# The second feed-forward layer: its first pair of hidden tiles by plain products instead of quarter sums, its second half of tokens as one block, and one PSUM pool

## The chip, the cores and the metric

The kernel runs on one core of one Trainium2 chip. The metric is the time of one execution on the device in microseconds. The time before is the median of three runs, 2837.39 us (2834.97 to 2839.1).

## The reference

Two layers of a diffusion transformer on 1024 tokens of width 1024, with a second small stream of 256 context tokens. Each layer is a mixer with a residual and then a gated feed-forward layer (FFN) with a residual, both on a normed and modulated input. The change touches the end of the second layer: its output projection, the norm behind it, and its FFN. In the reference that is

```
x = x + g_m * y                      # y = concat(fourier_mix, gla_output) @ w_out
h = rmsnorm(x, norm_ffn_w) * (1 + sc_f) + sh_f
x = x + g_f * ((silu(h @ w_gate) * (h @ w_up)) @ w_down)
return rmsnorm(x, final_norm_w)
```

with w_out 1024 x 1024 (half of its products lie earlier in the kernel), w_gate and w_up 1024 x 2816, w_down 2816 x 1024, all in float32.

## The kernel before, in words

**Layout.** x lies transposed in SBUF as eight tiles xT[k] of 128 features x 1024 tokens. Each factor of a product is split into a high and a low part of a shorter float (`split`: ScalarE casts the high part at L56, VectorE subtracts it at L57 for the low part), and one product is three matmuls (`mm3`, L49 to L51). XBLK is the pair of token blocks 0 to 511 and 512 to 1023.

**Seven products for eight.** Gate and up of this FFN are computed for two hidden tiles j and j+1 at a time (11 such pairs, j = 0, 2, ... 20) by a scheme of the Strassen kind: the 1024 x 1024 input is taken as four quarters (features 0 to 511 or 512 to 1023 by tokens 0 to 511 or 512 to 1023), and `quad` does seven products of sums of quarters in the order 1, 2, 5, 6, 7, 3, 4. Operands 1, 2, 4 and 5 are the quarters themselves (tiles called mixc and mixd in the trace), 6, 7 and 3 are sums of quarters, kept by `Sums` as tiles s, e and a. Each product has 12 matmuls of 512 columns into one PSUM bank (tile qp), and VectorE adds it up behind (L666; ScalarE copies the first, L677). The weights' sums are made by GpSimd (L619), split, and handed over by `Feed`, whose calls `take` and `ahead` set where in the program that work stands. Between gate and up of a pair lie the products with w_down of the pair before (`down_sums`, tile dn, residual into xT at L316).

**The stretch that is rewritten.** `out_sums` does the remaining half of the output projection (tile op) in three blocks of tokens, 512, 256 and 256 wide, four steps of two output tiles each. After each step `residual` (L316) adds into xT and `Squares.add` squares and sums (L433, L437). Generators are stepped between the steps: `norm_first` for the first block, `norm_second` for each of the other two. They turn the sums of squares into 1/rms (a matmul ss at L444, a diagonal at L447, a broadcast matmul rbc at L452), write the normed input (L457, L458) with its split, and also the sums of quarters 6, 7 and 3 (L470, L487 to L492). The first pair of hidden tiles needs those sums, so gate and up of j = 0 go by `quad` too, interleaved by hand with the last norm (`next(gate)`, `next(late)`, `next(up)`).

**PSUM.** Two pools follow one another. The first, `ps`, is closed behind the output projection (`pss.close()`), the second, `ps2`, opened for the FFN. In both, tag "s" is two tiles of two banks each, which `psum` hands out in halves, tags t, m and o are single banks. In `ps2` the products of `quad` have a tag of their own, "q", of four single banks, that also serves the final norm (`final`, tile ft).

**What sets the order.** A scheduler places each instruction by the order of the program and by its dependencies; it works by tiles. An engine runs its instructions in that order and stands at one whose semaphores are not there yet.

Of the kernel before, what the change touches and what calls it, by code (L numbers as in the profile page):

```python
# [388 lines left out]
class Sums:  # L389
# [5 lines left out]
    def __init__(self, pool):  # L395
        self.pool = pool
        self.s = {}
        raw = [self.new(f"a{i}", F32) for i in range(4)]
        self.a11 = [raw[k // 2][:, k % 2, :] for k in range(4)]
        self.a1s = [raw[2 + k // 2][:, k % 2, :] for k in range(4)]  # L400

    def new(self, tag, dt=F32R):
        return self.pool.tile([P, 2, 512], dt, name=tag, tag=tag, bufs=1)
# [20 lines left out]
class Squares:


    def __init__(self, s, blk):
        self.s, self.blk, self.acc = s, blk, None

    def add(self, xT, k):  # L430
        s, (o, n) = self.s, self.blk
        sq = scratch(s)[:, :n]
        s.nc.scalar.activation(sq, xT[k][:, o:o + n], AF.Square)  # L433
        if self.acc is None:
            self.acc = sq
        else:
            s.nc.vector.tensor_tensor(self.acc, self.acc, sq, ALU.add)  # L437

    def spread(self):

        s, n = self.s, self.blk[1]
        ss = psum(s, "m", "ss")
        for j in range(n // P):
            s.nc.tensor.matmul(ss[:, j:j + 1], self.acc[:, j * P:(j + 1) * P], s.ones[:, :1], start=True, stop=True)  # L444
        r = rsqrt(s, s.np_, ss[:, :n // P], 1.0 / D)
        dg = scratch(s)[:, :n]
        s.nc.vector.tensor_tensor(dg.rearrange("p (n q) -> p n q", n=n // P),  # L447
                                  s.ident.rearrange("p (o q) -> p o q", o=1).to_broadcast([P, n // P, P]),
                                  r.rearrange("p (n o) -> p n o", o=1).to_broadcast([P, n // P, P]), ALU.mult)
        yield  # L450
        self.bc = psum(s, "o", "rbc")[:, :n]
        s.nc.tensor.matmul(self.bc, s.ones, dg, start=True, stop=True)  # L452

    def normed(self, xT, k, l, dst):

        s, (o, n) = self.s, self.blk
        s.nc.vector.scalar_tensor_tensor(dst, xT[k][:, o:o + n], s.acol[l][1][:, k, 0:1], self.bc, ALU.mult, ALU.mult)  # L457
        s.nc.scalar.activation(dst, dst, AF.Identity, bias=s.mod[l][:, 24 + k, 0:1])  # L458


def norm_first(s, sq, xT, hT, S, l):

    yield from sq.spread()
    yield
    for k in range(KT):
        v = (S.a11 if k < 4 else S.a1s)[k % 4]
        sq.normed(xT, k, l, v)
        split(s, hT[k][0][:, :512], hT[k][1][:, :512], v, "pool" if k % 2 else "dve")
        if k >= 4:
            s.nc.gpsimd.tensor_tensor(v, v, S.a11[k - 4], ALU.add)  # L470
        if k % 2:
            yield


def norm_second(s, sq, xT, hT, S, l):

    nc = s.nc
    o, n = sq.blk
    sl = slice(o - 512, o - 512 + n)
    yield from sq.spread()  # L480
    yield
    for k in range(4):
        a, b = scratch(s), scratch(s)
        a21, a22, s1, s2 = a[:, :n], a[:, n:2 * n], b[:, :n], b[:, n:2 * n]
        sq.normed(xT, k, l, a21)
        sq.normed(xT, k + 4, l, a22)
        nc.vector.tensor_tensor(s1, a21, a22, ALU.add)  # L487
        nc.vector.tensor_tensor(s2, s1, S.a11[k][:, sl], ALU.subtract)
        for i, v, eng in ((5, s1, "dve"), (6, s2, "dve"), (4, a22, "pool")):
            split(s, *[x[:, sl] for x in S.operand(hT, i, k)], v, eng)  # L490
        nc.gpsimd.tensor_tensor(S.a11[k][:, sl], S.a11[k][:, sl], a21, ALU.subtract)
        nc.gpsimd.tensor_tensor(S.a1s[k][:, sl], S.a1s[k][:, sl], s1, ALU.subtract)  # L492
        yield


def norm_last(s, hT, S):

    last = scratch(s)
    for k in range(4):
        split(s, *S.operand(hT, 7, k), S.a11[k])  # L500
        yield
    s.nc.scalar.copy(last, S.a1s[3])
    for k in range(4):
        split(s, *S.operand(hT, 3, k), S.a1s[k] if k < 3 else last)
        yield


def early_weights(s, S, w, at):

    raw = s.wp.tile([P, KT, P], F32, name="wraw", tag="wraw", bufs=s.nraw)  # L510
    s.nc.sync.dma_start(raw, w[:, :P].rearrange("(k p) n -> p k n", p=P))
    units = []
    for x in range(2):
        hi, lo = S.early(at + x)
        split(s, hi, lo, raw[:, 4 * x:4 * x + 4, :].rearrange("p k n -> p (k n)"))
        units.append((hi, lo))
    return units


def out_sums(s, w, mix, xT, hT, S, l, order, early):  # L520


    q0, nq = min(order), len(order)
    weights = lambda k: wslab(s, w[q0 * P:(q0 + nq) * P, k * P:(k + 2) * P], nq, 2 * P)

    todo = [((0, 512), (0, 2, 4, 6)), ((512, 256), (2, 4, 6, 0)), ((768, 256), (0, 6, 4, 2))]
    steps = [(b, k0) for b, ks in todo for k0 in ks]
    load = {0: [0, 2], 1: [4], 2: [6], 4: [0], 8: [2]}
    kept = {}
    late = iter(())  # L530
    sq = None
    for i, (blk, k0) in enumerate(steps):
        o, n = blk
        if sq is None or sq.blk != blk:
            if sq is not None:
                late = norm_first(s, sq, xT, hT, S, l) if o == 512 else norm_second(s, sq, xT, hT, S, l)
            sq = Squares(s, blk)
        if i < 3:
            for c in load.get(i, ()):
                kept[c] = weights(c)  # L540
        if i == 9:
            early()
        wh, wl = kept[k0]
        ps = [psum(s, "s", "op") for _ in range(2)]

        for part in (order[:-1], order[-1:]):
            for x in range(2):
                c = slice(x * P, (x + 1) * P)
                for q in part:
                    mm3(s.nc, ps[x][:, :n], (wh[:, q - q0, c], wl[:, q - q0, c]),  # L550
                        (mix[q][0][:, o:o + n], mix[q][1][:, o:o + n]), q == order[0], q == order[-1])
        for x in range(2):
            residual(s, xT, k0 + x, blk, ps[x][:, :n], l, 2)
            sq.add(xT, k0 + x)
            next(late, None)
        if i >= 3:
            for c in load.get(i, ()):
                kept[c] = weights(c)
    for _ in late:
        pass  # L560
    return norm_second(s, sq, xT, hT, S, l)


# [49 lines left out]
def quarters(w, j, first=True):  # L613
# [4 lines left out]
    def job(feed):  # L618
# [3 lines left out]
        if first:  # L622
            for b in (b11, b21):
                feed.unit(b)
                yield 0
# [35 lines left out]
def quad(s, feed, xs, u, out, done, first=None):  # L661
# [21 lines left out]
    feed and feed.ahead()  # L683
    feed = (yield) or feed
# [19 lines left out]
class Hidden:  # L704


    def __init__(self, s, xs):
        self.s, self.xs = s, xs
        self.g, self.h = {}, {}

    def tile(self, tag, bufs=1, dt=F32):
        return self.s.fp.tile([P, 512], dt, name=tag, tag=tag, bufs=bufs)

    def gate(self, feed, first=None):
# [7 lines left out]
        return quad(self.s, feed, self.xs, self.tile("hu", 2), out, done, first)  # L722

    def up(self, feed, first=None):
# [3 lines left out]
        def done(y, x, c):  # L728
            h = self.g[y, x]
            self.s.nc.vector.tensor_tensor(h, h, c, ALU.mult)  # L730
            if self.s.fh:
                self.keep(y, x)

        return quad(self.s, feed, self.xs, self.tile("hu", 2), out, done, first)
# [28 lines left out]
def out_proj(s, w, mix, xT, l, blocks, order, places, behind):  # L763
# [1272 lines left out]
```

## Time and profile before

| | |
|---|---|
| Median of three runs | 2837.39 us |
| The profiled execution | 2844.29 us, span of the records 2842.5 us |
| TensorE busy | 2715.8 us, 96% of the span |
| VectorE, ScalarE, GpSimd busy | 1759.7, 969.4, 343.1 us |
| Granted TensorE clock, mean | 0.981 |
| From the first 256-wide op matmul (2101.55 us) to the first dn matmul (2222.07 us) | 120.52 us |

Times in the traces are microseconds from the start of the span. In a timeline a row has its start, its duration, engine, line, operation and output <- inputs, and in brackets how long the engine had been idle before it and who released it. A matmul's duration overlaps that of the next, so the distance between two starts is its price. In a table by windows each engine has its busy time with the number of instructions in brackets; PEclk is the share of full clock that TensorE was granted.

### The profile page before, as it was taken

The numbers are of one execution on the slowest core, as the hardware profiler recorded it, in microseconds if no ns is written. First come the engines' busy times: TensorE is split into PE (matmuls) and PEld (weight loads), VectorE is DVE, ScalarE is ACT, GpSimd is POOL, SyncE is SP. The second block draws the span as 40 slices with busy tenths as digits, with TensorE's granted clock in tenths as the row PEclk, the third lists the DMA queues.
The fourth block names the chain that finished last, engine by engine and source line by source line (L and its number), as shares of the span: only waits on it lengthen the run. The fifth ranks groups of instructions, "written<-read, shape, count | busy, mean of one in ns | idle before, by whom it ended". The sixth has DMA issues, their size and how long they took to land.

```text
span 2842.5 us, 39083 instructions
## 1 busy us (share of the span) xinstructions
PE 2715.8 (96%) x14761; PEld 2306.9 (81%) x14761; DVE 1759.7 (62%) x3138; ACT 969.4 (34%) x2102; POOL 343.1 (12%) x346
## 2 busy tenths in 40 slices
PE   8999899889999999999999999999997999999998
PEld 3889788777888888888888878788885888888887
DVE  5655677666664544646433474856677766667666
ACT  3442466554411111111111146465245322223222
POOL 0000122221100000000000020312014211112111
PEclk9999999999999999999999999999998999999999
DMA  8545655765132312213211143542641111121212
GB/s 304 163 129 152 183 163 163 216 197 158 59 119 60 97 55 80 85 50 97 82 38 45 38 142 91 144 146 69 188 137 50 53 59 52 45 60 45 67 52 82
DMA packets 265244, 299.59 MB, mean 105 GB/s; under 512 B 33448, under 2 KB 208225, under 8 KB 265057
## 3 DMA queue, kind: packets, MB, share of 16 engines
q1 hardware_dynamic: 265057, 297.10, 34.8%
q8 instruction: 117, 1.92, 0.3%
q14 instruction: 70, 0.57, 0.1%
HBM read 229.14 MB, written 64.49 MB: 103 GB/s over the span
## 4 chain that ended last, share of the span: by engine, by line
PE 79%; DVE 9%; ACT 4%; DMA 4%; issue 2%; POOL 1%; SPq 0%; DVEq 0%; POOLq 0%; ACTq 0%
PE pg L51 7%; PE pg L50 7%; PE pg L49 7%; PE dn L49 6%; PE dn L51 6%; PE dn L50 6%; PE qp L49 5%; PE qp L50 5%; PE qp L51 5%; PE o L1124 2%; DMA adaw<-in_ada_w_dram 2%; PE pt L1094 1%; DVE adaacc L183 1%; PE qk L49 1%; DVE wlo L57 1%
## 5 line engine op out<-in xcount | busy, mean ns | idle before, releaser
L56 ACT CAST whi<-wraw 128x512 fp32r<-128x512 f32 (+2 forms) x317 | 241.1, 765 | 735.5 <-PE dn L50 414.9
L57 DVE TENSOR_TENSOR wlo<-wraw,whi 128x512 fp32r<-128x512 f32 (+2 forms) x317 | 297.1, 939 | 141.0 <-ACT whi L56 139.5
L316 DVE SCALAR_TENSOR_TENSOR xT<-dn,mod,xT 128x512 f32<-128x512 f32 (+1 forms) x448 | 300.2, 685 | 126.0 <-PE dn L51 125.1
L49 PE MATMUL dn<-hhi,whi 128*128 128x512 f32 (+1 forms) x896 | 328.3, 368 | 6.5 <-DVE xT L316 4.9
L50 PE MATMUL dn<-hlo,whi 128*128 128x512 f32 (+1 forms) x896 | 326.7, 365 | 0.0
L51 PE MATMUL dn<-hhi,wlo 128*128 128x512 f32 (+1 forms) x896 | 326.5, 365 | 0.0
L51 PE MATMUL pg<-hh,wlo 128*128 128x512 f32 x688 | 269.2, 391 | 1.0 <-DVE wlo L57 1.0
L49 PE MATMUL pg<-hh,whi 128*128 128x512 f32 x688 | 269.0, 391 | 0.0
L50 PE MATMUL pg<-hl,whi 128*128 128x512 f32 x688 | 268.3, 390 | 0.0
L183 DVE SCALAR_TENSOR_TENSOR adaacc<-adaw,cs,adaacc 128x1024 f32<-128x1024 f32 x140 | 174.9, 1280 | 117.5 <-DMA adaw<-in_ada_w_dram 114.7
L49 PEld LDWEIGHTS dn<-hhi,whi 128*128 128x128 f32 x896 | 168.9, 189 | 39.3 <-DVE xT L316 10.6
L51 PEld LDWEIGHTS dn<-hhi,wlo 128*128 128x128 f32 x896 | 168.9, 188 | 27.1
L50 PEld LDWEIGHTS dn<-hlo,whi 128*128 128x128 f32 x896 | 169.0, 189 | 26.5
L619 POOL TENSOR_TENSOR wraw<-wraw 128x512 f32<-128x512 f32 x88 | 125.3, 1424 | 496.9 <-DVE wlo L57 309.6
L345 ACT ACTIVATE sg<-pg 128x512 f32<-128x512 f32 (+1 forms) x66 | 34.5, 523 | 360.4 <-PE pg L51 360.3
L346 DVE TENSOR_TENSOR sg<-sg,pg 128x512 f32<-128x512 f32 (+1 forms) x66 | 39.2, 593 | 187.8 <-ACT sg L345 187.8
L51 PEld LDWEIGHTS pg<-hh,wlo 128*128 128x128 f32 x688 | 129.4, 188 | 28.6 <-DVE wlo L57 1.8
L50 PEld LDWEIGHTS pg<-hl,whi 128*128 128x128 f32 x688 | 129.5, 188 | 26.0
L49 PEld LDWEIGHTS pg<-hh,whi 128*128 128x128 f32 x688 | 129.5, 188 | 26.0
L275 POOL TENSOR_TENSOR sqacc<-sqacc,sq 128x512 f32<-128x512 f32 (+1 forms) x14 | 17.0, 1217 | 903.9 <-ACT sq L274 902.8
L1051 POOL TENSOR_SCALAR y<-y,sst 128x768 f32<-128x768 f32 (+2 forms) x80 | 71.7, 897 | 261.2 <-DVE sst L1050 133.7
L50 PE MATMUL pg<-hc,whi 128*128 128x256 f32 x344 | 96.7, 281 | 0.0
(625 smaller groups left out, 6734.2 us busy)
## 6 DMA issues: line engine op xcount, KB each, us to landing
adaw<-in_ada_w_dram SPq DMA_DIRECT2D x96, 512.0 KB, 3.9
wraw<-in_ffn_w_gate_dram SPq DMA_DIRECT2D x45, 512.0 KB, 3.9
wraw<-in_ffn_w_up_dram SPq DMA_DIRECT2D x45, 512.0 KB, 3.8
wraw<-in_ffn_w_down_dram SPq DMA_DIRECT2D x44, 512.0 KB, 3.8
wraw<-in_ab_w_in_dram SPq DMA_DIRECT2D x20, 512.0 KB, 6.0
xd<-xT SPq DMA_DIRECT2D x16, 640.0 KB, 6.6
xs<-xd SPq DMA_DIRECT2D x32, 256.0 KB, 3.4
xd<-xs SPq DMA_DIRECT2D x32, 256.0 KB, 2.9
```

The lines of the kernel that those rows point to most:

```text
L49: nc.tensor.matmul(out, wh, xh, start=start, stop=False)
L50: nc.tensor.matmul(out, wh, xl, start=False, stop=False)
L51: nc.tensor.matmul(out, wl, xh, start=False, stop=stop)
L56: s.nc.scalar.copy(hi, src)
L57: (s.nc.gpsimd if eng == "pool" else s.nc.vector).tensor_tensor(lo, src, f32(hi), ALU.subtract)
L183: nc.vector.scalar_tensor_tensor(acc[:, v], w, c, acc[:, v], ALU.mult, ALU.add)
L316: s.nc.vector.scalar_tensor_tensor(xT[k][:, o:o + n], ps, s.mod[l][:, 8 * vec + k, sel:sel + 1], xT[k][:, o:o + n], ALU.mult, ALU.add)
L345: nc.scalar.activation(sg[:, :n], pg[:, :n], AF.Silu)
L346: nc.vector.tensor_tensor(sg[:, :n], sg[:, :n], pu[:, :n], ALU.mult)
L619: sub = lambda out, x, y: feed.s.nc.gpsimd.tensor_tensor(out, x, y, ALU.subtract)
L1051: nc.gpsimd.tensor_scalar(y[:, :256 + xn], y[:, :256 + xn], st[:, 5:6], 1.0, ALU.mult, ALU.mult)
L1124: nc.tensor.matmul(o_ps[:, ba * P:bz * P], vv[:n, kt, :], at(x, sl)[:n, 0, ba:bz, :].rearrange("p b q -> p (b q)"), start=q == 0 and x == ...
```

## The change

1. `out_sums` goes; the output projection is done by `out_proj`, which the other places of the kernel use already, with two blocks of 512 tokens. `Norm.add` is called behind each residual. The weights of the first two steps are read again for the second block, into places where the quarter sums lie later (`S.places`, tiles s0 to s3).
2. Gate and up of j = 0 are plain products (`H.plain`, tile pg, eight products of 24 matmuls each, 192 in place of 168). For the first half of tokens their weights are split early (`early_weights`, tile e, for gate; `whole` for up). For the second half gate and up are interleaved and take the normed tiles in the order 0, 4, 1, 5, 2, 6, 3, 7. The norm of the second block is one of 512 tokens (L459, L464 to L468), and the quarter sums are made behind it, `sums()` and `rest()` in the program.
3. The operand 3 is made from operand 6: a12 + shift - s2, one VectorE instruction.
4. One PSUM pool is left. The tag "q" is gone: a product of `quad` takes a half of a two-bank tile of tag "s" (of which there are two), and `final` takes such a tile for its two halves.

Line numbers move: the adds of `quad` are at L648 after, the copy at L657, ss at L448, the diagonal at L258, rbc at L261, the norm's product at L459.

```diff
 def psum(s, tag, name=None):
     if tag != "s":
-        return s.ps.tile([P, 512], F32, name=name or tag, tag=tag, bufs={"t": 2, "q": 4}.get(tag, 1))
+        return s.ps.tile([P, 512], F32, name=name or tag, tag=tag, bufs=2 if tag == "t" else 1)
...
+    def tile(self, k, dst, hT, eng="dve"):
+        s, (o, n) = self.s, self.blk
+        s.nc.vector.scalar_tensor_tensor(dst, self.xT[k][:, o:o + n], s.acol[self.l][1][:, k, 0:1], self.bc,
+                                         ALU.mult, ALU.mult)
+        hi, lo = [x[:, o:o + n] for x in hT[k]]
+        if eng == "pool":
+            t = scratch(s)
+            s.nc.scalar.activation(t, dst, AF.Identity, bias=self.shift(k))
+            split(s, hi, lo, t, "pool")
+        else:
+            s.nc.scalar.activation(hi, dst, AF.Identity, bias=self.shift(k))
+            s.nc.vector.scalar_tensor_tensor(lo, dst, self.shift(k), f32(hi), ALU.add, ALU.subtract)
+
+def norm_first(s, N, hT, S):
+    N.spread()
     for k in range(KT):
-        v = (S.a11 if k < 4 else S.a1s)[k % 4]
-        sq.normed(xT, k, l, v)
-        split(s, hT[k][0][:, :512], hT[k][1][:, :512], v, "pool" if k % 2 else "dve")
-        if k >= 4:
-            s.nc.gpsimd.tensor_tensor(v, v, S.a11[k - 4], ALU.add)
-        if k % 2:
-            yield
+        N.tile(k, S.raw[k], hT, "pool" if k % 2 else "dve")
...
+            stt(s2, a22, N.shift(k), a11, ALU.subtract, ALU.subtract)
+            split(s, *S.operand(hT, 6, k), s2)
+            stt(a12, a12, N.shift(k + 4), s2, ALU.add, ALU.subtract)
...
 def quad(s, feed, xs, u, out, done):
     def product(i):
-        ws = first.pop(0) if first else feed.take()
-        ps = psum(s, "q", "qp")
+        hi, lo = feed.take()
+        ps = psum(s, "s", "qp")
...
+    def plain(self, ws, hT, y):
+        nc = self.s.nc
+        o = 512 * y
+        for mats in ((0, 1),) if y else ((0,), (1,)):
+            ps = {m: [psum(self.s, "s", "pg") for _ in range(2)] for m in mats}
+            for k in KORDER if y else range(KT):
+                for m in mats:
+                    for x in range(2):
+                        hi, lo = ws[m][x][k // 4]
+                        c = slice(k % 4 * P, k % 4 * P + P)
+                        mm3(nc, ps[m][x], (hi[:, c], lo[:, c]), [h[:, o:o + 512] for h in hT[k]], k == 0, k == KT - 1)
...
-                pt = [psum(s, "q", "ft") for _ in range(2)]
+                pt = psum2(s, "ft")
...
+    def behind(blk):
+        if blk == XBLK[0]:
+            norm_first(s, norms_[blk], hT, S)
+            ws.append(early_weights(s, S, wg))
+
+    out_proj(s, a["cd_w_out"][0], mix, xT, 1, XBLK, [0, 1, 2, 3], S.places(), behind, lambda blk, k: norms_[blk].add(k))
     wps.close()
-    pss.close()
-    s.ps = pool("ps2", space=PSUM)
...
+    H = Hidden(s)
+    sums, rest = norm_second(s, norms_[XBLK[1]], hT, S)
+    H.plain(ws, hT, 0)
+    H.plain(ws, hT, 1)
     dump("x3", xT, T)
-    for _ in norm_last(s, hT, S):
-        feed.ahead()
+    sums()
+    rest()
```

The order of instructions at two places. First, VectorE's order around the norm of the first block (L457 before and L459 after write the normed tile from xT, acol and rbc; L57 and L468 make the low part; L316 is the residual of the output projection's next block). Before:

```order
L457 SCALAR_TENSOR_TENSOR a_19268<-xT_19241,acol_182,rbc 128x512 [waits DMAHW5_49,PE_49]
L316 SCALAR_TENSOR_TENSOR xT_19245<-op,mod_178,xT_19245 128x256 [waits DMAHW0_49,PE_49]
L457 SCALAR_TENSOR_TENSOR a_19268<-xT_19242,acol_182,rbc 128x512
L437 TENSOR_TENSOR nt<-nt 128x256 [waits Activation_49]
L316 SCALAR_TENSOR_TENSOR xT_19246<-op,mod_178,xT_19246 128x256
L57 TENSOR_TENSOR mixc<-a_19268,mixc 128x512 [waits Activation_49]
```

and after, the rows from the first norm product to the next block's first residuals:

```order
L459 SCALAR_TENSOR_TENSOR a_19269<-xT_19243,acol_182,rbc 128x512
L468 SCALAR_TENSOR_TENSOR mixc<-a_19268,mod_178,mixc 128x512 [waits Activation_49]
L459 SCALAR_TENSOR_TENSOR a_19269<-xT_19244,acol_182,rbc 128x512
L468 SCALAR_TENSOR_TENSOR mixc<-a_19269,mod_178,mixc 128x512 [waits Activation_49]
L459 SCALAR_TENSOR_TENSOR a_19270<-xT_19245,acol_182,rbc 128x512
L459 SCALAR_TENSOR_TENSOR a_19270<-xT_19246,acol_182,rbc 128x512
L459 SCALAR_TENSOR_TENSOR a_19271<-xT_19247,acol_182,rbc 128x512
L468 SCALAR_TENSOR_TENSOR mixd<-a_19270,mod_178,mixd 128x512 [waits Activation_49]
L459 SCALAR_TENSOR_TENSOR a_19271<-xT_19248,acol_182,rbc 128x512
L468 SCALAR_TENSOR_TENSOR mixd<-a_19271,mod_178,mixd 128x512 [waits Activation_49]
L316 SCALAR_TENSOR_TENSOR xT_19245<-op,mod_178,xT_19245 128x512 [waits DMAHW0_49,PE_49]
L316 SCALAR_TENSOR_TENSOR xT_19246<-op,mod_178,xT_19246 128x512
```

The residuals of the second block stood between the norm's instructions before; now they stand behind all twelve of them (two L459 rows stand ahead of this piece).

Second, TensorE's order in an up of the steady part, at the seam from product 6 (operand s) to product 7 (operand e), with the numbers of the tiles. Before:

```order
L49 MATMUL qp_20626<-s3_19806,whi_20556 128x512
L50 MATMUL qp_20626<-s3_19806,whi_20556 128x512
L51 MATMUL qp_20626<-s3_19806,wlo_20557 128x512
L49 MATMUL qp_20647<-e0_20020,whi_20577 128x512 [waits Activation_49]
L50 MATMUL qp_20647<-e0_20020,whi_20577 128x512
L51 MATMUL qp_20647<-e0_20020,wlo_20578 128x512 [waits DVE_49]
```

and after:

```order
L49 MATMUL qp_20817<-s3_19946,whi_20749 128x512
L50 MATMUL qp_20817<-s3_19946,whi_20749 128x512
L51 MATMUL qp_20817<-s3_19946,wlo_20750 128x512
L49 MATMUL qp_20817<-e0_19958,whi_20769 128x512 [waits DVE_49,Activation_49]
L50 MATMUL qp_20817<-e0_19958,whi_20769 128x512
L51 MATMUL qp_20817<-e0_19958,wlo_20770 128x512
```

Products 6 and 7 had tiles of their own and now are the halves of one tile, and the first matmul of product 7 has got a wait for VectorE, whose add (L648) reads the first half of that tile.

More of the change, by code (lines that the diff above doesn't have):

```diff
@@ L397, in __init__, with new, places @@
         self.s = {}
[L398 to L403, printed above, removed]
+        raw = [self.new(f"a{i}", dt=F32) for i in range(4)]
+        self.raw = [raw[k // 2][:, k % 2, :] for k in range(KT)]
+    def new(self, tag, shape=(P, 2, 512), dt=F32R):
+        return self.pool.tile(list(shape), dt, name=tag, tag=tag, bufs=1)
+    def places(self):
+        for i in (0, 2):
+            yield [self.new(f"s{i + x}", (P, 4, 2 * P)) for x in range(2)]
     def early(self, i):
@@ L439, in spread @@
     def spread(self):
-        s, n = self.s, self.blk[1]
-        ss = psum(s, "m", "ss")
-        for j in range(n // P):
+        s = self.s
+        ss = psum(s, s.nbanks[0], "ss")
+        for j in range(4):
             s.nc.tensor.matmul(ss[:, j:j + 1], self.acc[:, j * P:(j + 1) * P], s.ones[:, :1], start=True, stop=True)
[L445 to L449, printed above, removed]
@@ L475, in norm_second @@
-def norm_second(s, sq, xT, hT, S, l):
-    nc = s.nc
[L478 to L493, printed above, removed]
@@ L496, in norm_last @@
[L496 to L517, printed above, removed]
@@ L520, in out_sums @@
[L520 to L551, printed above, removed]
-        for x in range(2):
[L553 to L561, printed above, removed]
@@ new lines, in spread, with shift @@
+        r = rsqrt(s, s.np_, ss[:, :4], 1.0 / D)
+        self.bc = psum(s, s.nbanks[1], "rbc")
+        spread(s, s.np_, r, self.bc, dg=scratch(s))
+    def shift(self, k):
+        return self.s.mod[self.l][:, 24 + k, 0:1]
+    def tile(self, k, dst, hT, eng="dve"):
+        s, (o, n) = self.s, self.blk
+        s.nc.vector.scalar_tensor_tensor(dst, self.xT[k][:, o:o + n], s.acol[self.l][1][:, k, 0:1], self.bc,
[8 more added lines that the diff above has]
+            s.nc.vector.scalar_tensor_tensor(lo, dst, self.shift(k), f32(hi), ALU.add, ALU.subtract)
@@ new lines, in norm_first, with norm_second, sums, last @@
+def norm_first(s, N, hT, S):
+    N.spread()
+    for k in range(KT):
+        N.tile(k, S.raw[k], hT, "pool" if k % 2 else "dve")
+KORDER = (0, 4, 1, 5, 2, 6, 3, 7)
+def norm_second(s, N, hT, S):
+    nc = s.nc
+    N.spread()
+    raw = {}
+    for k in KORDER:
+        raw[k] = scratch(s)
+        N.tile(k, raw[k], hT)
+    def sums():
+        both = s.np_.tile([P, 8], F32, name="both")
+        nc.vector.tensor_tensor(both[:, :4], s.mod[N.l][:, 24:28, 0], s.mod[N.l][:, 28:32, 0], ALU.add)
+        stt = nc.vector.scalar_tensor_tensor
+        for k in range(4):
+            a11, a12, a21, a22 = S.raw[k], S.raw[k + 4], raw[k], raw[k + 4]
+            stt(a22, a21, both[:, k:k + 1], a22, ALU.add, ALU.add)
+            nc.gpsimd.tensor_tensor(a21, a11, a21, ALU.subtract)
+            s2 = scratch(s)
+            stt(s2, a22, N.shift(k), a11, ALU.subtract, ALU.subtract)
+            split(s, *S.operand(hT, 6, k), s2)
+            stt(a12, a12, N.shift(k + 4), s2, ALU.add, ALU.subtract)
+    def last():
+        for i in (5, 7):
+            for k in range(4):
+                split(s, *S.operand(hT, i, k), raw[k + 4 if i == 5 else k])
+        keep = scratch(s)
+        nc.scalar.copy(keep, S.raw[7])
+        for k in range(4):
+            split(s, *S.operand(hT, 3, k), S.raw[k + 4] if k < 3 else keep)
+    return sums, last
@@ new lines, in early_weights @@
+def early_weights(s, S, w):
+    ws = [[], []]
+    for half in range(2):
+        raw = s.wp.tile([P, 4, 2 * P], F32, name="wraw", tag="wraw", bufs=s.nraw)
+        s.nc.sync.dma_start(raw, w[512 * half:512 * (half + 1), :2 * P].rearrange("(k p) n -> p k n", p=P))
+        for x in range(2):
+            hi, lo = S.early(2 * half + x)
+            split(s, hi.rearrange("p (k n) -> p k n", k=4), lo.rearrange("p (k n) -> p k n", k=4),
+                  raw[:, :, P * x:P * (x + 1)])
+            ws[x].append((hi, lo))
+    return ws
@@ L621, in job @@
         sub(t, t, b11)
[L622 to L625, printed above, removed]
+        for b in (b11, b21):
+            feed.unit(b)
+            yield 0
         feed.unit(t)
@@ L642, in quarters, with whole, job @@
     return job, loads
+def whole(w, j):
+    loads = [w[512 * x:512 * (x + 1), j * P:(j + 2) * P].rearrange("(k p) n -> p k n", p=P) for x in range(2)]
+    def job(feed):
+        for _ in range(2):
+            raw = feed.raw()
+            for x in range(2):
+                feed.unit(raw[:, :, P * x:P * (x + 1)])
+                if x:
+                    feed.load()
+                yield 0
+    return job, loads
 def rows(w, j):
@@ L658, in rows, with quad @@
     return job, loads
-def quad(s, feed, xs, u, out, done, first=None):
+def quad(s, feed, xs, u, out, done):
     nc = s.nc
@@ L682, in quad @@
     done(0, 0, c)
-    feed and feed.ahead()
-    feed = (yield) or feed
+    feed.ahead()
     p5 = product(5)
@@ L704, with __init__, gate @@
 class Hidden:
-    def __init__(self, s, xs):
-        self.s, self.xs = s, xs
+    def __init__(self, s):
+        self.s = s
         self.g, self.h = {}, {}
     def tile(self, tag, bufs=1, dt=F32):
-        return self.s.fp.tile([P, 512], dt, name=tag, tag=tag, bufs=bufs)
-    def gate(self, feed, first=None):
+        pool = self.s.fh if tag == "hu" else self.s.fp
+        return pool.tile([P, 512], dt, name=tag, tag=tag, bufs=bufs)
+    def gate(self, feed, xs):
         def out(y, x):
@@ L720, in done, with up @@
             self.s.nc.scalar.activation(c, c, AF.Silu)
-        return quad(self.s, feed, self.xs, self.tile("hu", 2), out, done, first)
-    def up(self, feed, first=None):
+        quad(self.s, feed, xs, self.tile("hu", 2), out, done)
+    def up(self, feed, xs):
         def out(y, x):
@@ L728, in done, with times @@
         def done(y, x, c):
[L729 to L734, printed above, removed]
+            self.times(y, x, c)
+            self.keep(y, x)
+        quad(self.s, feed, xs, self.tile("hu", 2), out, done)
+    def plain(self, ws, hT, y):
[5 more added lines that the diff above has]
+                for m in mats:
+                    for x in range(2):
+                        hi, lo = ws[m][x][k // 4]
+                        c = slice(k % 4 * P, k % 4 * P + P)
+                        mm3(nc, ps[m][x], (hi[:, c], lo[:, c]), [h[:, o:o + 512] for h in hT[k]], k == 0, k == KT - 1)
+            for x in range(2):
+                if 0 in mats:
+                    self.g[y, x] = self.tile("ua" if (y, x) == (1, 0) else f"g{y}{x}")
+                    nc.scalar.activation(self.g[y, x], ps[0][x], AF.Silu)
+                if 1 in mats:
+                    self.times(y, x, ps[1][x])
+    def times(self, y, x, c):
+        h = self.g[y, x]
+        self.s.nc.vector.tensor_tensor(h, h, c, ALU.mult)
     def keep(self, y, x):
@@ L760, in down_sums, with out_proj @@
             behind([(o, n)])
-def out_proj(s, w, mix, xT, l, blocks, order, places, behind):
+def out_proj(s, w, mix, xT, l, blocks, order, places, behind, each=None):
     q0, nq = min(order), len(order)
@@ L1765, in dump @@
                 nc.sync.dma_start(dbg[name][k * P:(k + 1) * P, :n], t[:, :n])
-    pss = ctx.enter_context(ExitStack())
-    s.ps = pss.enter_context(P_("ps", space=PSUM))
+    s.ps = pool("ps", space=PSUM)
     s.half = s.bg = None
@@ L1940, in body @@
     feed = Feed(s, jobs + [rows(wd, HT - 2)])
-    next(late)
-    feed.ahead(1)
-    next(up)
-    for _ in late:
-        feed.ahead(1)
+    units = [feed.take() for _ in range(4)]
+    ws.append([[[u.rearrange("p k n -> p (k n)") for u in units[2 * half + x]] for half in range(2)] for x in range(2)])
+    H = Hidden(s)
+    sums, rest = norm_second(s, norms_[XBLK[1]], hT, S)
+    H.plain(ws, hT, 0)
+    H.plain(ws, hT, 1)
     dump("x3", xT, T)
-    for _ in norm_last(s, hT, S):
-        feed.ahead()
+    sums()
+    rest()
     nps.close()
     s.fh = pool("fp3", side="right")
-    H.keep(0, 0)
-    def rest(steps):
-        try:
-            steps.send(feed)
-        except StopIteration:
-            pass
-    rest(gate)
-    rest(up)
+    for y in range(2):
+        for x in range(2):
+            H.keep(y, x)
+    xs = lambda i, k: S.operand(hT, i, k)
     for j in range(2, HT, 2):
-        last, H = H, Hidden(s, xs)
-        for _ in H.gate(feed):
-            pass
+        last, H = H, Hidden(s)
+        H.gate(feed, xs)
         down_sums(s, feed, xT, last.h, 1)
-        for _ in H.up(feed):
-            pass
+        H.up(feed, xs)
     sps.close()
```

57 lines of the change are left out of this document (19 added, 38 removed).

## The prediction

> **What bounds the kernel now.** I read the page first, then stretches of the span, then the timeline at TensorE's gaps, since the page leaves little but TensorE:
>
> ```profile
> span 2842.5 us, 39083 instructions
> PE 2715.8 (96%) x14761; PEld 2306.9 (81%) x14761; DVE 1759.7 (62%) x3138; ACT 969.4 (34%) x2102; POOL 343.1 (12%) x346
> ```
>
> The stretches (after the span of each: its length, then busy time of PE, PEld, DVE, ACT and POOL, the granted clock, DMA):
>
> ```profile
> 2104.83:2136.62 31.79, 26.68 (x183) 24.95 (x183) 28.40 (x50) 19.08 (x38) 14.83 (x11) 0.89 0.12 35
> 2136.62:2151.30 14.68, 0.00 (x0) 0.03 (x1) 12.57 (x23) 6.63 (x18) 11.42 (x12) 0.59 0.23 71
> 2151.30:2181.55 30.25, 25.52 (x86) 17.60 (x86) 23.71 (x41) 15.61 (x35) 15.76 (x19) 0.86 0.06 18
> 2205.20:2813.00 607.80, 607.80 (x2685) 503.02 (x2684) 418.93 (x575) 168.70 (x283) 112.14 (x79) 1.00 0.18 53
> ```
>
> The last row is the steady part: TensorE has no gap in 607.8 us, 607.80 / 2685 = 0.2264 us for a matmul of 512 columns, at full clock. Whatever the change adds in waits there is paid in full. The three rows above are the rewritten stretch; it holds gaps and half clock. Its ends, its largest gap and the row that ends it:
>
> ```profile
> 2101.55 0.28 PE L49 MATMUL op<-mixc,whi 128*128 128x256 f32 x1
> 2101.67 0.28 PE L50 MATMUL op<-mixc,whi 128*128 128x256 f32 x1
> 2150.73 0.47 DVE L457 SCALAR_TENSOR_TENSOR nt<-xT,acol,rbc 128x256 f32<-128x256 f32 x1
> 2151.30 0.77 PE L49 MATMUL qp<-mixc,e 128*128 128x512 f32 x1 [14.69 <-issue]
> 2222.07 0.39 PE L49 MATMUL dn<-hhi,whi 128*128 128x512 f32 x1
> ```
>
> The stretch takes 2222.07 - 2101.55 = 120.5 us. The first qp starts 0.10 us after the last L457 of the second block has ended (2150.73 + 0.47): that instruction is the last reader of rbc, a tile of the pool that is closed here, so the 14.69 us is the pool's change waiting for the second block's norm. The other waits of TensorE in it, from the view of waits and the timeline:
>
> ```profile
> PE ss L444 <- DVE nt L437: 2.3, 1, 2.3
> PE qp L50 <- DVE mixc L57: 2.9, 3, 1.0
> 2117.42 0.48 DVE L316 SCALAR_TENSOR_TENSOR xT<-op,mod,xT 128x256 f32<-128x256 f32 x1
> 2117.95 0.39 PE L49 MATMUL op<-mixc,whi 128*128 128x256 f32 x1 [1.99 <-DVE xT L316]
> ```
>
> The last two also give the restart: 2117.95 - 2117.90 = 0.05 us from VectorE's end to the next matmul. Work without gaps would be 192 x 0.12 (2101.55 to 2101.67) + 252 x 0.2264 (168 of j = 0, 84 of the gate of j = 2) + about 4 for ss and rbc = 84 us; 36 us are lost.
>
> **The rewritten stretch after.** Matmuls: 96 op, 192 pg and the 84 of the next gate, all of 512 columns: 372 x 0.2264 = 84.2 us. The plain products cost 24 matmuls (5.4 us) more than the sevenfold scheme; the blocks of 512 cost 21.7 in place of 23.0. Prices for the rest:
>
> ```profile
> 2127.17 0.58 PE L444 MATMUL ss<-ones,nt 128*128 128x1 f32 x4 [2.32 <-DVE nt L437]
> 2163.54 0.70 PE L452 MATMUL rbc<-nt,ones 128*128 128x256 f32 x2 [0.89 <-DVE nt L447]
> 2117.81 1.40 DVE L457 SCALAR_TENSOR_TENSOR a<-xT,acol,rbc 128x512 f32<-128x512 f32 x2
> L57 DVE TENSOR_TENSOR wlo<-wraw,whi 128x1024 fp32r<-128x1024 f32 x2 | 2.4, 1214 | 0.0
> ```
>
> - ss and rbc, two norms: 2 x (0.58 + 0.70) and some 0.3 of draining at each of the four: 4 us, an estimate, as before.
> - First ss: two 1024-wide low parts of 1.21 us stand on VectorE ahead of the last residuals and sums of squares; between nothing and 2.4, I take 1.4. The two rbc wait for rsqrt and diagonal, 0.89 in the row; I take 0.7 each.
> - The third op step of the second block takes the two-bank tile whose last reader is the residual of xT5. In VectorE's order that residual, the second of two, stands behind all twelve instructions of the first norm: 14 x 0.70 = 9.8 us after rbc. TensorE has 26 matmuls left by then, 5.9 us. The stall is 3.9 us, and what is queued behind it are all later op and pg matmuls. Bounds: 0, if VectorE keeps ahead (it does not stand elsewhere), and 6, if the low parts on it wait for ScalarE.
> - A gap of that size costs half a clock window (3.43 us at half clock, see below): 1.7, between 0 and 3.4.
> - The pool's change is gone, and pg of the first half needs only the first norm, done by then. The second norm (8 x 0.70, low parts, ss without stall) lies beside 96 pg matmuls, 21.7 us. Its sums, with their low parts some 40 instructions of VectorE of 0.7 us, 28 us, lie beside the second 96 (21.7 us) and the products 1, 2 and 5 of the next gate (36 matmuls, 8.2 us). That cover of 30 us is thin; the next gate's product 6 is what would be late. I put 0.3 there, between 0 and 6.
>
> Sum: 84.2 + 4 + 1.4 + 1.4 + 3.9 + 1.7 + 0.3 = 96.9 us against 120.5: **23.6 us less**, between 16 and 32.
>
> **The steady part after.** Here the change of tags tells. In an up of the present kernel, at the ends of products 6 and 7 (TensorE and VectorE rows of the timeline, then the whole group):
>
> ```profile
> 2314.32 0.39 PE L51 MATMUL qp<-s,wlo 128*128 128x512 f32 x1
> 2314.55 0.39 PE L49 MATMUL qp<-e,whi 128*128 128x512 f32 x1
> 2314.75 0.69 DVE L666 TENSOR_TENSOR hu<-qp,hu 128x512 f32<-128x512 f32 x1 [0.48 <-PE qp L51]
> 2317.04 0.39 PE L51 MATMUL qp<-e,wlo 128*128 128x512 f32 x1
> 2317.27 0.39 PE L49 MATMUL qp<-a,whi 128*128 128x512 f32 x1
> 2317.47 0.69 DVE L666 TENSOR_TENSOR hu<-qp,hu 128x512 f32<-128x512 f32 x1 [0.49 <-PE qp L51]
> L666 DVE TENSOR_TENSOR hu<-qp,hu 128x512 f32<-128x512 f32 x58 | 40.0, 689 | 44.6 <-PE qp L51 44.5
> ```
>
> Product 7 starts 0.23 us after the last matmul of 6, beside the add. If it must wait for the add, it starts at 2314.75 + 0.69 + 0.05 = 2315.49 and not at 2314.55: 0.94 us lost. The same at the next seam: 2317.47 + 0.69 + 0.05 - 2317.27 = 0.94. VectorE stood idle ahead of both adds, so nothing delays them now.
>
> Which seams wait: 14 products of a gate and an up fill seven tiles, and the tiles in an up are (4 of the gate, 1), (2, 5), (6, 7), (3, 4). Product 7 writes the tile that the add of 6 reads; the tile (3, 4) goes where the add of 7 has just freed one. Both have no other matmul between. With ten ups that is 20, less two in the last up, where dn matmuls stand between: 18 x 0.94 = 16.9 us. Of those two, one has two matmuls between (0.94 - 2 x 0.2264 = 0.5). Some 31 further waits (2 to 5, 7 to 3 in the gates, the dn behind) have four matmuls between, 0.91 of 0.94 us: 0.03 each, or 0.2 where VectorE is at another instruction: 3. The start of each gate behind product 4's add, with six between: 0.15 each, 1.5. Sum: **22 us more**. Bounds: 15 (the 18 alone, some of them covered) and 30 (each add 0.4 late behind a low part of the weights).
>
> Its loads are two fewer (before two early and four by `Feed` for j = 0, after two and two; six for the projection in both): hidden, DMA being 0.18 busy in the steady row. GpSimd loses its quarter sums (12% busy in all): nothing waits for it there. The S4 instruction is one VectorE instruction of 0.7 us for a GpSimd add: in the sums above.
>
> **The tail.** `final` takes one tile for two halves, so the transposes of the second half wait for the square of the first:
>
> ```profile
> L1685 ACT ACTIVATE fsq<-ft 128x512 f32<-128x512 f32 x16 | 9.4, 596 | 20.7 <-PE ft L1683 14.6 <-issue 6.1
> ```
>
> Eight tiles at 0.6 us, most with other matmuls between, the last ones not: 1 us, between 0 and 3.
>
> **Sum.** -23.6 + 22 + 1 = -0.6 us. The profiled execution took 2844.29, 6.9 above the median; the sum is a difference, and I set it against the median: 2837.39 - 0.6, 2837 us. For this kernel 0.2% is 5.7 us, about what a measurement can tell from no change.
>
> **A rule that speaks against the change.** The clock as the trace shows it, in three neighbouring windows of 3.43 us:
>
> ```profile
> 2166.66:2170.09 3.43, 2.22 (x9) 1.15 (x7) 3.43 (x7) 1.48 (x4) 2.04 (x3) 1.00 0.00 0
> 2170.09:2173.52 3.43, 2.01 (x7) 0.93 (x6) 3.43 (x7) 2.20 (x5) 2.42 (x3) 1.00 0.00 0
> 2173.52:2176.95 3.43, 3.43 (x9) 2.20 (x8) 3.03 (x6) 2.97 (x7) 1.86 (x4) 0.50 0.00 0
> ```
>
> A window with 2.22 us of PE work left the next at full clock, one with 2.01 us brought half clock. In the steady part after, two seams are 12 matmuls (2.7 us) apart, so no window holds more than one whole gap: 3.43 - 0.8 = 2.6 us of work, above both. I take full clock. The Trainium skill, "TensorE: Matmul & The Clock Gate", section "A second HAM failure mode: psum-queue depth-cycling", says otherwise of a kernel that cycles through PSUM banks: the small idles between groups of matmuls were frequent enough to make the clock swing between half and full. By that rule the time would be that of rival 3.
>
> **The rivals.**
> 1. Faster, the wait is not on the add. The order marks that product 7 waits for VectorE, not for which instruction; were it an older one (a low part of weights), the 18 seams cost nothing. For: the order before shows such marks at product 3, with no gap. Against: 6 and 7 write one tile, and dependencies go by tiles. -23.6 + 5 + 1: 2820 us.
> 2. Faster, the stretch runs without its stalls: no 3.9, no 1.7, no 2.8 at the norms. For: VectorE was 28.4 of 31.8 us busy with the old, longer list. Against: the residual stands where the order shows it. 8.4 less: 2828 us.
> 3. Slower, the clock swings in the steady part: each up loses one half-clock window, 1.7 us, ten times: 2837 + 17 = 2854 us. It decides if a window with 2.6 us of work is counted as idle; the first row above speaks against it.
> 4. Slower, VectorE is the bound at the seams and in the sums: adds start 0.4 late behind low parts of weights (8 us at 20 seams), and the second gate's product 6 waits 3 us for its operands: 2848 us. For: the thin cover of 30 us. Against: the idle 0.48 us ahead of the adds.
> 5. The change does not take the gap away but moves it to the third op step: 3.9 becomes 14 if that step also waits for its reloaded weights, queued behind the early gate weights: 2848 us. Against: these loads are issued in the first block.
>
> **How the numbers follow.** Chances: forecast with its bounds (2828 to 2846) 0.60; rival 1 0.08, rival 2 0.12, rival 3 0.07, rivals 4 and 5 0.13 together. The forecast's own spread puts about 0.43 within 0.2%, 0.08 below and 0.09 above. With the rivals: faster 0.08 + 0.08 + 0.12 = 0.28; slower 0.09 + 0.07 + 0.13 = 0.29; same 0.43. The range of 2825 to 2851 leaves out rivals 1 and 3 and a little at the ends, under 2 in 10.
>
> **What would show it.** In the trace after: no gap of 14 us at the output projection's end; one of about 4 us ahead of an op matmul, released by L316; the first dn some 97 us behind the first op matmul of the second block; in each up two gaps of 0.75 us on TensorE ahead of qp with e and with a, released by L648; the clock at 1.00 in the steady part. I am wrong if those gaps are missing or larger than 1 us, if the clock falls there, or if the gate of j = 2 stands for its operands s, e or a.

## The result and the profile after

The changed kernel takes 2872.32 us, median of four runs (2871.06 to 2875.75), against 2838.18 for the kernel before on the same chip: a ratio of 1.0124, 95% interval 1.0107 to 1.0142. It is 34 us slower; 2837 with a range to 2851 was forecast. Its profiled execution took 2872.18 us, span 2870.2.

The same three stretches by windows (columns as above: length, busy time of PE, PEld, DVE, ACT, POOL, clock, DMA). Before, the rewritten stretch, the steady part and the tail:

```profile
2101.55:2222.07 120.52, 95.71 (x468) 77.89 (x466) 100.02 (x162) 61.14 (x123) 53.06 (x47) 0.89 0.16 48
2222.07:2812.54 590.47, 590.47 (x2606) 488.61 (x2605) 404.30 (x555) 161.30 (x270) 107.36 (x76) 1.00 0.18 52
2812.54:2842.50 29.96, 20.49 (x161) 18.44 (x159) 20.07 (x49) 10.33 (x32) 4.34 (x8) 0.89 0.38 141
```

After, from the first op matmul of the second block to the first dn, on to the first ft, and to the end:

```profile
2091.91:2195.08 103.17, 90.80 (x370) 71.72 (x368) 75.09 (x104) 42.42 (x71) 20.37 (x14) 0.93 0.09 29
2195.08:2840.47 645.39, 608.74 (x2628) 489.30 (x2629) 386.73 (x561) 165.33 (x274) 107.46 (x76) 1.00 0.16 49
2840.47:2870.20 29.73, 20.95 (x161) 18.72 (x159) 20.43 (x49) 10.80 (x32) 4.36 (x8) 0.87 0.38 142
```

After, dn begins ahead of the gate's last two products, so 24 matmuls (5.4 us) have moved from the first row to the second. Like for like the stretch takes 103.2 + 5.4 = 108.6 us, 11.9 less than before; the steady part 645.4 - 5.4 = 640.0, **49.5 more**; the tail 0.2 less. That is +37.4, of which the medians show 34. The stretch begins at 2101.55 in the one execution and at 2091.91 in the other, though TensorE has 11531 instructions ahead of it in both: that part varies by some us from execution to execution (its mean granted clock was 0.98 in the one and 0.99 in the other), which is why stretches and not spans are compared here.

Who kept TensorE waiting in the steady part, in the view of waits after (sum, times, longest):

```profile
PE qp L49 <- DVE hu L648: 15.8, 18, 0.9
PE qp L49 <- ACT hu L657: 10.7, 9, 1.3
PE qp L49 <- DVE ua L648: 9.7, 10, 1.0
```

The first row is what the prediction counted, 18 gaps at the seams 6 to 7 and 7 to 3. One of them in the timeline:

```profile
2299.67 0.39 PE L51 MATMUL qp<-s,wlo 128*128 128x512 f32 x1
...
2300.10 0.69 DVE L648 TENSOR_TENSOR hu<-qp,hu 128x512 f32<-128x512 f32 x1
...
2300.94 0.47 PE L49 MATMUL qp<-e,whi 128*128 128x512 f32 x1 [0.88 <-DVE hu L648]
```

From start to start it is 1.27 us in place of 0.23. The other two rows were not foreseen. The seam from 2 to 5 in an up, GpSimd to TensorE:

```profile
2291.90 1.29 POOL L586 TENSOR_TENSOR wraw<-wraw 128x512 f32<-128x512 f32 x1 [0.69 <-DVE wlo L57]
...
2292.97 0.39 PE L51 MATMUL qp<-mixd,wlo 128*128 128x512 f32 x1
...
2293.22 1.14 ACT L56 CAST whi<-wraw 128x512 fp32r<-128x512 f32 x2 [1.96 <-POOL wraw L586]
...
2293.88 0.69 DVE L57 TENSOR_TENSOR wlo<-wraw,whi 128x512 fp32r<-128x512 f32 x1 [2.12 <-ACT whi L56]
2294.49 0.68 DVE L648 TENSOR_TENSOR ua<-qp,hu 128x512 f32<-128x512 f32 x1
...
2295.23 0.50 PE L49 MATMUL qp<-mixc,whi 128*128 128x512 f32 x1 [0.97 <-DVE ua L648]
```

(The two casts, and likewise other rows marked x2 or more, are merged in this view.) Product 2 was done at 2293.36 (2292.97 + 0.39). Its add stood on VectorE behind a low part of weights, that behind its cast, that behind GpSimd's sum of weights. The add ended at 2295.17, and product 5, the other half of the same tile, started then. Four matmuls in between (0.9 us) did not cover it. The same at the seam from 1 to 2 in a gate, with ScalarE's copy as the reader (ten matmuls of product 5 in between):

```profile
2314.95 0.62 ACT L56 CAST whi<-wraw 128x512 fp32r<-128x512 f32 x1 [2.63 <-POOL wraw L586]
2315.47 0.61 ACT L56 CAST hhi<-hu 128x512 fp32r<-128x512 f32 x1
2315.99 0.57 ACT L657 COPY hu<-qp 128x512 f32<-128x512 f32 x1
2316.62 0.50 PE L49 MATMUL qp<-mixd,whi 128*128 128x512 f32 x1 [1.17 <-ACT hu L657]
```

The adds are not later than they were. In the kernel before, the same add:

```profile
2308.88 0.39 PE L51 MATMUL qp<-mixd,wlo 128*128 128x512 f32 x1
2309.11 0.39 PE L49 MATMUL qp<-mixc,whi 128*128 128x512 f32 x1
...
2309.79 0.69 DVE L57 TENSOR_TENSOR wlo<-wraw,whi 128x512 fp32r<-128x512 f32 x1 [2.12 <-ACT whi L56]
2310.40 0.68 DVE L666 TENSOR_TENSOR ua<-qp,hu 128x512 f32<-128x512 f32 x1
```

It started 1.13 us after its product had ended, as after (2294.49 - 2293.36), behind the same cast; product 5 had a bank of its own and started at 2309.11. Four tiles hid this lateness, and the change uncovered it.

In the stretch, the larger gaps after are 2.0 us ahead of ss, and these two (each with the VectorE instruction that, as read below, ended it):

```profile
2113.35 2.71 DVE L316 SCALAR_TENSOR_TENSOR xT<-op,mod,xT 128x512 f32<-128x512 f32 x4
...
2114.85 0.76 PE L49 MATMUL op<-mixc,s 128*128 128x512 f32 x1 [4.64 <-ACT whi L56]
...
2156.63 1.27 DVE L735 TENSOR_TENSOR g<-g,pg 128x512 f32<-128x512 f32 x2
...
2157.95 0.50 PE L49 MATMUL pg<-mixc,whi 128*128 128x512 f32 x1 [3.68 <-DVE g L735]
```

The op step starts some 0.1 us after the second of the four residuals (2113.35 + 2 x 0.68 = 2114.71). The row names a cast on ScalarE that ended 0.3 us before the step (it started at 2113.94), but that cast is of weights of w_up, which the step does not read; the last experiment comes back to this. The pg of the second half waits for the last reader of a pg tile of the first half, a multiply that stands on VectorE behind the second norm and the first of the quarter sums.

### The profile page after: what moved, and what is told of

It reads as the page before. It is cut to its first block, busy times and chain, and to the rows that moved or that the text cites. A ratio compares the mean times of both kernels' runs of the same rounds, so it can differ in the third digit from the quotient of the medians.

```text
span 2870.2 us, 38742 instructions
## 1 busy us (share of the span) xinstructions
PE 2721.8 (95%) x14687; PEld 2292.9 (80%) x14687; DVE 1722.3 (60%) x3090; ACT 959.6 (33%) x2058; POOL 311.5 (11%) x313
## 5 line engine op out<-in xcount | busy, mean ns | idle before, releaser
L56 ACT CAST whi<-wraw 128x512 fp32r<-128x512 f32 (+2 forms) x309 | 234.8, 767 | 743.7 <-PE dn L50 406.0
L316 DVE SCALAR_TENSOR_TENSOR xT<-dn,mod,xT 128x512 f32<-128x512 f32 (+1 forms) x448 | 299.9, 686 | 122.1 <-PE dn L51 121.2
L57 DVE TENSOR_TENSOR wlo<-wraw,whi 128x512 fp32r<-128x512 f32 (+2 forms) x309 | 280.3, 912 | 149.5 <-ACT whi L56 149.3
L51 PEld LDWEIGHTS dn<-hhi,wlo 128*128 128x128 f32 x896 | 168.9, 188 | 27.5 <-DVE wlo L57 0.4
L586 POOL TENSOR_TENSOR wraw<-wraw 128x512 f32<-128x512 f32 x80 | 113.5, 1418 | 552.5 <-DVE wlo L57 381.9
L51 PE MATMUL pg<-hc,wlo 128*128 128x256 f32 x344 | 96.7, 281 | 0.0
```

Source lines behind the costliest of these rows:

```text
L51: nc.tensor.matmul(out, wl, xh, start=False, stop=stop)
L56: s.nc.scalar.copy(hi, src)
L57: (s.nc.gpsimd if eng == "pool" else s.nc.vector).tensor_tensor(lo, src, f32(hi), ALU.subtract)
L316: s.nc.vector.scalar_tensor_tensor(xT[k][:, o:o + n], ps, s.mod[l][:, 8 * vec + k, sel:sel + 1], xT[k][:, o:o + n], ALU.mult, ALU.add)
L586: sub = lambda out, x, y: feed.s.nc.gpsimd.tensor_tensor(out, x, y, ALU.subtract)
```

## The experiments

Theory A: the loss is qp products sharing two-bank tiles, and the rest of the change is a gain. Theory B: the steady part is slower for another reason. For the seams nobody had foreseen, C1: the reader stands in its queue behind weights that GpSimd has not summed; C2: VectorE and ScalarE have too much to do.

**The change without its PSUM part.**

```diff
-        return s.ps.tile([P, 512], F32, name=name or tag, tag=tag, bufs=2 if tag == "t" else 1)
+        return s.ps.tile([P, 512], F32, name=name or tag, tag=tag, bufs={"t": 2, "q": 4}.get(tag, 1))
-        ps = psum(s, "s", "qp")     # pg and ft likewise
+        ps = psum(s, "q", "qp")
     wps.close()
+    pss.close()
+    s.ps = pool("ps2", space=PSUM)
```

> The changed kernel with the PSUM of before for the FFN: the first pool closed behind the output projection, the second with four single banks "q" for qp, pg and ft. Theory A (all of the loss is qp products sharing two-bank tiles, and the rest of the change gains what the stretch shows, 21.6 us): no gap in the steady part, 2838 - 21.6 and 0 to 5 us for the pool's change, 2816 to 2822 us. Theory B (the steady part is slower for another reason, the phase of the weight feed or the places of tiles in SBUF, and the seams only show it): gaps stay under other names, 2850 us or more.

Measured: 2822.00 us, ratio to before 0.9936 (0.9921 to 0.9951). Stretch and steady part:

```profile
2091.55:2198.00 106.45, 95.68 (x394) 75.72 (x392) 78.82 (x108) 43.11 (x72) 23.44 (x14) 0.94 0.10 30
2198.00:2788.47 590.47, 590.47 (x2606) 488.61 (x2604) 405.15 (x557) 162.43 (x273) 107.50 (x76) 1.00 0.18 53
```

The steady part is to the hundredth that of before, without a gap. Theory A holds, B falls: with the weight feed and the places as changed, banks of their own in a second pool are enough. The stretch is worth 120.5 - 106.5 = 14.1 us. (The 21.6 in the expectation was counted from 2101.55 in both executions and is wrong by the 9.6 us by which the stretch began earlier. With 14.1 in its place the range would have been 2824 to 2829, so that the time lies on the upper end of the one written down, 2822, is luck; the medians put the gain at 16.7.)

**The PSUM part alone, on the kernel before.**

```diff
-        ps = psum(s, "q", "qp")     # ft likewise
+        ps = psum(s, "s", "qp")
-    pss.close()
-    s.ps = pool("ps2", space=PSUM)
```

> The kernel before with one edit: one PSUM pool, qp and ft in halves of two-bank tiles. Theory A: the steady part loses the same 47 us and the tail 2; the 14.7 us gap of the pool's change and its half clock go, but the quads of j = 0 get seam waits of their own: 2838 + 49 - 18 + 0 to 15, 2868 to 2884 us. Theory B: the steady part stays without gaps, 2820 to 2838 us.

Measured: 2901.48 us, ratio 1.0226 (1.0204 to 1.0248).

```profile
2105.74:2233.28 127.54, 98.04 (x444) 76.09 (x442) 97.43 (x157) 59.29 (x119) 53.26 (x47) 0.84 0.14 42
2233.28:2881.59 648.31, 609.14 (x2629) 488.94 (x2628) 389.41 (x560) 165.37 (x274) 107.89 (x76) 1.00 0.16 48
```

The steady part loses 648.3 - 5.4 - 590.5 = 52.4 us (it too starts dn ahead of the gate's end), as theory A says, and more than the 47 expected. The time is 17 us over my range, and the stretch was misjudged: it did not get 18 us shorter with the pool's change gone, but 7 longer. (The tail came out 0.5 us shorter, and not 2 longer.) The gap of 14.7 us is replaced by smaller ones at the quads of j = 0, whose readers stand behind the second block's norm (one wait for L666 of 5.5 us, two for the copy, 3.7 us) and ahead of ss and rbc (4.6 and 2.0 us), and the clock is 0.84. What the pool's change costs by itself this run does not show, since the shared tiles came with its end.

**The change without GpSimd's sums of weights.**

```diff
-        sub = lambda out, x, y: feed.s.nc.gpsimd.tensor_tensor(out, x, y, ALU.subtract)
+        sub = lambda out, x, y: None
```

> The changed kernel without GpSimd's sums of the weights' quarters (the products take the plain quarters, so the FFN computes something else). Theory C1 (the seams from 2 to 5 and from 1 to 2, together 23.4 us, wait because the reader on VectorE or ScalarE stands in its queue behind a split of weights that GpSimd has not summed yet): those two gaps go, those from 6 to 7 and 7 to 3 stay at 0.9 us, 2872 - 23 = 2849 us. Theory C2 (the readers are late since VectorE and ScalarE have too much to do): the gaps shrink by less than half, 2862 us or more.

Measured: 2852.58 us, ratio 1.0047 (1.0032 to 1.0062), against 2849 for C1 and over 2862 for C2. All of the waits of qp that are left in the steady part:

```profile
PE qp L49 <- DVE hu L648: 14.9, 18, 0.9
```

and the add that was late, in the timeline:

```profile
2291.75 0.69 DVE L648 TENSOR_TENSOR ua<-qp,hu 128x512 f32<-128x512 f32 x1 [1.67 <-PE qp L51]
```

The add of product 2 now waits for TensorE and not in the queue. The waits at the two unforeseen seams are gone but for 0.1 us from start to start, the two foreseen ones are as they were: C1. The adds take 0.69 us with and without GpSimd's sums, so it is their place in the queue and not their speed that GpSimd set.

**Tiles that begin with each quad.** One line makes them (1, 2), (5, 6), (7, 3), (4) in gates and ups.

```diff
+    s.half = None
     nc.scalar.copy(u, product(1))
```

> The changed kernel with one line more: each quad starts a new two-bank tile, so that the tiles are (1, 2), (5, 6), (7, 3), (4) in gates and ups alike. Theory A with C1: in the ups the gaps from 2 to 5 and from 6 to 7 go (20.7 us), the one from 7 to 3 stays; in the gates 4 and not 10 matmuls now lie between product 1 and 2, so that gap grows from 1.35 to 2.7 us (12 us more) and, being over 2 us in a window of 3.43, may bring half clock (up to 15 more): 2864 us, or 2879 with half clock. Theory B: no change, 2872 us.

Measured: 2849.23 us, ratio to before 1.0030 (1.0015 to 1.0044), 23 us under the changed kernel, and better than I expected.

```profile
PE qp L49 <- DVE hu L648: 7.9, 9, 0.9
PE qp L49 <- ACT hu L658: 4.5, 9, 0.5
```

The seams 2 to 5 and 6 to 7 of the ups are gone, as A says. The gap in the gates shrank to 0.5 us and did not grow to 2.7. The order that the scheduler makes has changed there: the copy (2315.51) now stands ahead of the next cast and not behind it, and that cast is the one that waits for GpSimd:

```profile
2314.99 0.62 ACT L56 CAST hhi<-hu 128x512 fp32r<-128x512 f32 x1 [1.90 <-DVE hu L736]
2315.51 0.58 ACT L658 COPY hu<-qp 128x512 f32<-128x512 f32 x1
2317.51 0.62 ACT L56 CAST whi<-wraw 128x512 fp32r<-128x512 f32 x1 [1.42 <-POOL wraw L586]
```

**Three single banks, and two,** for qp, pg and ft in place of four ("q": 3, "q": 2 in the first experiment's line).

> Run e1_singles with three single banks for qp in place of four. Theory A in its sharper form (a seam costs only where a matmul's tile was read within the last product; sharing a tile does that, few tiles need not): each product now has a whole product (12 matmuls, 2.7 us) between it and the reader that it waits for; the latest reader measured is 3.2 us late, so a gap of at most 0.5 us in a gate, 2822 to 2830 us. If it is the number of banks that counts, three are worse than the four of the changed kernel: over 2872 us.

> Run e1_singles with two single banks for qp. Product 5 keeps one of them until its second add, so products 6, 7 and 3 follow one another in the other: two gaps of 0.9 us in each up, as in the changed kernel, and, with a whole product between, none of note from 1 to 2 and from 2 to 5. Theory A, sharper form: 2822 + 19 and 0 to 10 us in the gates, 2841 to 2851 us, faster than the changed kernel with half of its banks. If the number of banks counts: over 2890 us.

Measured: 2832.91 us with three, ratio 0.9976 (0.9964 to 0.9988); 2872.46 with two, 1.0122 (1.0108 to 1.0135). The steady part with three:

```profile
2205.89:2796.35 590.46, 590.46 (x2606) 488.61 (x2604) 404.85 (x556) 161.34 (x270) 107.51 (x76) 1.00 0.18 53
```

and with two, with the waits of TensorE from there to the end:

```profile
2204.76:2835.71 630.95, 609.38 (x2641) 493.45 (x2642) 389.64 (x562) 165.28 (x274) 105.83 (x76) 1.00 0.17 50
```

```profile
PE qp L49 <- DVE hu L648: 15.8, 18, 0.9
PE dn L49 <- ACT whi L56: 9.3, 11, 3.5
PE ft L1686 <- DVE fo L1694: 8.9, 7, 2.7
```

Three single banks have no gap in the steady part, where the changed kernel with four banks in two tiles has 37: the number of banks is not what counts. (The time is 3 us over my range; the tail is 2 us longer, and the stretch began 7 us later than in the first experiment.) With two the quads wait just as forecast, 18 times, none at 1 to 2 or 2 to 5: for these 18 waits two shared tiles are no better than two single banks, and the other 19 of the changed kernel come only with the sharing. But my 2841 to 2851 missed two other waits: dn, placed early between products, stands for its weights (9.3 us), and the transposes of the final norm for their tiles (8.9 us). Two single banks come out like the changed kernel, by other waits in part.

**The first norm between the residuals,** on the first experiment: two tiles of the first norm behind each step of the second block.

```diff
-            norm_first(s, norms_[blk], hT, S)
+            norms_[blk].spread()
...
+    def each(blk, k):
+        norms_[blk].add(k)
+        if blk == XBLK[1] and k % 2:
+            for i in (next(todo), next(todo)):
+                norms_[XBLK[0]].tile(i, S.raw[i], hT, "pool" if i % 2 else "dve")
```

> Run e1_singles with the first block's norm tiles emitted two at a time behind each step of the projection's second block, and not all ahead of it. Theory D (the gap of 3 to 5 us ahead of the third op step is the residual of xT5 behind the whole first norm on VectorE): that gap of 3.1 us and the half clock behind it go, 4.5 us in all, 2817 us. Theory E (the step waits for its weights, loaded again): the gap stays, 2822 us.

Measured: 2821.03 us, ratio 0.9932 (0.9919 to 0.9945); against the first experiment's 2822.00 no difference that these runs can tell.

```profile
2095.99:2198.97 102.98, 93.99 (x394) 75.04 (x393) 77.64 (x108) 43.30 (x72) 21.01 (x14) 0.95 0.11 31
```

```profile
2127.03 0.47 PE L49 MATMUL pg<-mixc,e 128*128 128x512 f32 x1 [2.83 <-ACT nt L437]
```

The gap ahead of the op step is gone (theory D; E would have kept it), and the stretch is 3.5 us shorter in the profile. The cast that the changed kernel's row named is ruled out by the first experiment's trace, where the step starts before it:

```profile
2113.56 0.77 PE L49 MATMUL op<-mixc,s 128*128 128x512 f32 x1 [3.10 <-issue]
...
2114.32 0.62 ACT L56 CAST whi<-wraw 128x512 fp32r<-128x512 f32 x1 [2.11 <-DMA wraw<-in_ffn_w_up_dram]
```

A part moved: the first pg, which is the first matmul of the new pool, now waits 2.8 us, 1.6 in the first experiment. These two versions are the fastest of the study, 17 to 19 us under the kernel before.

## Why the prediction was wrong

The sum is off by 38 us: 27.5 in the steady part (49.5 for 22), 11.7 in the stretch, and 1.2 the other way in the tail. **The step that failed is, first, one term of the steady part**: "some 31 further waits ... 0.03 each, or 0.2 ...: 3", with the 1.5 for the gates' starts. It makes 18.9 of the 38 (23.4 for 4.5). The ten seams 2 to 5 cost 11.3 us from start to start, and the nine seams 1 to 2 in the gates, which I had not listed because ten matmuls lie in between, 12.1. I sized the cover by the handoff of 0.94 us, measured at two seams where VectorE sat idle ahead of the add. At the two others the reader is later by the queue ahead of it. The trace of before had it: 2310.40 is not 2308.88 + 0.39 + 0.04. I had looked at the adds that nothing delays, and took them for all. With this term alone put right the forecast would have been 2856 us, still outside of its range; the second step that failed is in the stretch, below.

**Right:** the 18 gaps with nothing in between, forecast at 0.94 us each; they are 0.88 idle and 1.04 from start to start. The restart is 0.15 us at these seams (2300.94 - 2300.79), not the 0.05 taken from an op matmul; at the two unforeseen ones it is 0.06 (2295.23 - 2295.17). The matmul behind a gap is slower: the next one starts 0.31 to 0.33 us after it and not 0.23. The 37 gaps cost 42.1 us from start to start, the slower matmuls behind them 3.6; the remaining 4 of the 49.5 are delays of 0.7 us and less, most of them at dn.

**The stretch:** forecast 96.9 us, measured 108.6, so its gain was 11.9 and not 23.6, below the 16 to 32 that I had allowed. The op stall came about as forecast (4.6 for 3.9), ss 2.0 for 1.4. Two terms failed. I had put nothing for a wait of pg on the readers of pg, and pg waits 3.7 us behind L735 (2.9 in the first experiment, with single banks, so the sharing is not what makes it wait). And for the clock I had 1.7, half of one window, where a mean of 0.93 over 103 us can cost up to 7. **The tail:** forecast +1, measured -0.2.

**The rivals.** Rival 4 named the mechanism, readers late behind low parts of weights, but at 11 us and with the thin cover of the sums as its reason; the gate's operands s, e and a were not late. Rival 1 is refuted by the 18 gaps. Rival 2 is refuted by the op stall and by a stretch that was longer than forecast. Rival 3 as well: the clock is 1.00 in the steady part after, with 37 gaps of 0.9 to 1.3 us idle. So the Trainium skill's case of a clock that swings when a kernel cycles through PSUM banks ("TensorE: Matmul & The Clock Gate", "A second HAM failure mode: psum-queue depth-cycling") did not come about here. Rival 5 fell: the op step waited 4.6 us, and for the residual.

The reason given against rival 3 was thinner than it reads. Two windows, 2.22 us of work and 2.01, were taken as the two sides of a bound. The same trace has a window with less work than either that was followed by full clock, so the bound does not come out of it:

```profile
637.53:640.94 3.41, 1.58 (x13) 1.58 (x14) 3.19 (x10) 1.33 (x6) 0.00 (x0) 1.00 0.85 303
640.94:644.36 3.42, 3.42 (x27) 3.07 (x26) 2.63 (x11) 2.29 (x7) 0.83 (x1) 1.00 0.93 272
```

That no window of the steady part fell to half clock is what was measured; how much idle time it would have taken is open.

## What to carry to other kernels

Before taking buffers away, read in the present trace how late each reader starts after its product has ended, for every seam and not for one: in these runs this lateness cost nothing while there was a spare buffer, and what the matmuls in between did not cover was paid when there was none. Two products that share a tile are serialized by its reader even in banks of their own, since the program's dependencies go by tiles; three single banks did here what four in two tiles did not. What stands ahead of the reader in its engine's queue, here a cast that waits for GpSimd, belongs to the price of the seam.

## What the runs showed of the hardware

TensorE was not back at once after a wait. At the 18 seams from 6 to 7 and from 7 to 3 it started 0.15 us after VectorE's add had ended, at the other 19 some 0.06 us after the add or copy. At the first of these seams the order above shows the matmul waiting for two engines; whether that is the reason was not tested. The matmul behind a gap was followed after 0.31 to 0.33 us and not 0.23.

TensorE's 11531 instructions ahead of the rewritten stretch, the same number in the changed kernel as before, ended between 2091.6 and 2105.7 us in these profiled executions, which is more than several of the effects measured here.
